# A recurrence on one Trainium2 core: y's matmuls in two groups, centring by a matmul, loads in other places, and output weights that are split once and read back split

## The chip, the core and the metric

The kernel runs on one core of one Trainium2 chip. The metric is device microseconds of one execution of the whole program. TensorE (PE) does matmuls into PSUM; VectorE (DVE) and ScalarE (ACT) work elementwise and are the ones that read PSUM here; GpSimd (POOL) works elementwise in SBUF and issues some DMAs; SyncE (SP) issues most DMAs, in the order of the program. All data are float32. A product of a weight and an activation is made of three matmuls, since both are split into a high and a low part (`h` and `l`): `wh*xh`, `wl*xh`, `wh*xl`.

## What is computed

One step of a two-layer decoder for a prompt of 1040 tokens and for 8 single tokens that share all weights. Layer 0 is retention and an RG-LRU, layer 1 is RWKV-7; each is followed by a gated ConvFFN. The change lies in layer 1, whose core is this recurrence over tokens, for 16 heads of 64:

```
def rwkv7_step(S, inp):
    r_t, w_t, k_t, v_t, a_t, b_t = inp
    sa = jnp.einsum('bhij,bhj->bhi', S, a_t)
    S = S * w_t[:, :, None, :] + sa[..., None] * b_t[:, :, None, :] + v_t[..., None] * k_t[:, :, None, :]
    y = jnp.einsum('bhij,bhj->bhi', S, r_t)
    return S, y
...
    mu = jnp.mean(ys, axis=-1, keepdims=True)
    var = jnp.mean(jnp.square(ys - mu), axis=-1, keepdims=True)
    o = ((ys - mu) * lax.rsqrt(var + GN_EPS_C)).reshape(B, T, D) * gn_g + gn_b
    bonus = jnp.sum(rh * kh * r_k, axis=-1, keepdims=True) * vh
    o = (o + bonus.reshape(B, T, D)) * g
    return o @ p['w_o'], ...
```

## The kernel before

Layer 1 has two parts. `Layer1A` makes r, k, v and the gates, writes what the recurrence needs to scratch in DRAM (`d_kq`, `d_vt`, `d_gg`, `d_ab`), and steps the 8 sample tokens' states (`samp_pair`, eight times for two heads each). `Layer1B` then runs the recurrence in 17 chunks of 64 tokens. A chunk is two units of work, f=0 and f=1, each for four pairs of heads, so there are 34 units; here they are counted 0 to 33. The order of steps in a unit is a string: `UNIT = "pa z pt g1 u r r o r p2 g2 o o s o r y p3"`. Each letter calls one function:

- `pa`, `pt`, `p2`, `p3` prepare the next unit (`prep1` and so on). The 16 matmuls of `pa` (tile `A`) open a unit in the trace.
- `z`, `u`, `s`, `y` are the steps of the recurrence. `y` (function `yy`) makes 16 matmuls into one PSUM tile `y`: for each of four pairs of heads two that contract over 64 rows (`s0v` by `kq`) and then two that contract over 128 rows (`uv` by `ly`).
- `g1`, `g2` normalise the y of the unit before (`gn_unit`, `gn_unit2`): mean by a matmul with ones (`bones`), subtraction on DVE (L1847), Square on ACT, mean of squares by a matmul (L1857), a reciprocal root on ACT and DVE, the product (L1357), gains, and the split into `yh`, `yl`.
- `r` is one step of the inversion of 32x32 triangular matrices (`inv_steps`), elementwise work on DVE (L1440, L1442). It goes through four batches of matrices (a fifth was done before), each loaded from `d_ab` on POOL's queue; the load of the next batch stands with the last step of the batch before.
- `o` is a quarter of one output tile: 6 matmuls of 256 to 272 columns with `w_o` (`out_steps`). Four blocks of tokens, eight tiles each. The first three blocks are woven in, one tile to a unit: block 0 in units 9 to 16, block 1 in 17 to 24, block 2 in 25 to 32. The fourth runs behind the recurrence in `finish`, back to back, with matmuls for the next norm behind each tile.

Weights go through a queue `wq`: `load_next` issues a DMA of 512 KB into one of two buffers `wst`, `split_next` splits it into one of two pairs `wh`, `wl` (ACT L323, DVE L324) and calls `load_next`. At the first `o` of a tile `next_w` splits the weights of the tile after it. `w_o` is read and split again in each of the four blocks.

SP's order in a chunk: at the end of unit f=1 the set of 13 loads of the chunk after the next (`kq` of 1 MB first; it waits until y is done with the same buffer), then in unit f=0 one `wst`, `gg` of the next chunk, then in f=1 another `wst`. `p.x` (the residual, 4.3 MB) is read back from `d_x` at the start of the recurrence, behind the sets of chunks 0 and 1 and `gg` of chunk 0. The buffers of `Layer1A` lie in the same memory.

Of the kernel before, what the change touches and what calls it, by code (L numbers as in the profile page):

```python
# [44 lines left out]
def constants():  # L45

    f = np.float32
    c = {}
# [128 lines left out]
def unlayout(o):  # L177
# [21 lines left out]
       0.69, "v.s2": 1.38, "v.sum": 4.97, "v7.pair": 2.3, "v7.post": 8.2, "v7.post_d": 0.01, "v.fold": 1.57, "v.tr0":  # L199
# [848 lines left out]
class Layer1A:  # L1048
# [464 lines left out]
    def samp_pair(self, m):  # L1513
        nc = self.nc
        tt = (nc.vector if m == 7 else nc.gpsimd).tensor_tensor
        S, (a, w, b, k, r) = self.samp_tiles(m)
# [46 lines left out]
    def run(self, pool, done, first):  # L1563
# [24 lines left out]
        for name, tile, nxt, temps in stages:  # L1588
            for m in range(8):
                f, new = tile(m)  # L1590
                if name == "v":
# [7 lines left out]
                    if m == 7:  # L1599
                        new.append((POS["v7.pair"] - 6, lambda: (self.samp_pair(7), self.samp_sum(7))))  # L1600
# [32 lines left out]
def w_order_l1(io):  # L1633
# [3 lines left out]
    return o + [io["w_o"][m] for _ in OBLK for m in range(8)]  # L1637
# [9 lines left out]
class Layer1B:  # L1647
# [189 lines left out]
    def gn_unit(self, u):  # L1837
# [8 lines left out]
        nc.tensor.matmul(py[:, 1], lhsT=p.bones, rhs=yf, start=True, stop=True)  # L1846
        nc.vector.scalar_tensor_tensor(out=yf, in0=py[:, 1], scalar=-1.0 / 64, in1=yf, op0=OP.mult, op1=OP.add)  # L1847
        sq, v, y = new("sq"), new("v"), new("yr")
        nc.scalar.activation(out=sq, in_=yf, func=AF.Square)
# [37 lines left out]
    def run(self, pool):  # L1887
# [75 lines left out]
def build(tc, io):  # L1963
    nc = tc.nc
    with ExitStack() as ctx:
# [93 lines left out]
def scratch(pool):  # L2059
# [33 lines left out]
```

## Time and profile before

| what | us |
|---|---|
| median of 3 runs (3443.21 to 3454.74) | 3443.9 |
| the profiled execution, its own time | 3447.01 |
| its span in the trace | 3445.2 |
| recurrence, units 0 to 33 (from 2221.82 in the trace) | about 380 |
| output tiles of the last block, behind it | about 31 |

The page's second part shows PE at 9 tenths or more of nearly every slice outside the stretch from 1900 to 2330. In that stretch DVE and the DMA engines are busiest, and the granted clock of PE falls now and then. Matmul ends are modelled, so a busy PE is not one at its peak: whether PE or another engine sets the pace of a unit is read from the idle times in brackets and from the distance between the same instruction of two units.

### The profile page before, as it was taken

The page shows a single profiled execution, that of the slowest core. Times are in us where ns is not written, and L with a number is a line of the kernel's source. Part 1 is how long each engine was busy: PE and PEld are TensorE (multiplying, and loading weights), DVE is VectorE, ACT ScalarE, POOL GpSimd, SP SyncE. Part 2 cuts the span into 40 slices and gives each one's busy share as a digit, 9 for nine tenths or more (in the row PEclk, how much of TensorE's full clock was granted, in tenths as well). Part 3 has the DMA queues.
Part 4 walks back from the last instruction along what each step waited for, and adds up shares of the span by engine and source line. Part 5 has one row for each costly group of instructions (what it writes and reads, how often), then busy time and mean ns, then how long its engine had stood idle before and what let it go on. Part 6 is the DMA issues. An engine that isn't in the chain of part 4 may idle for free.

```text
span 3445.2 us, 55808 instructions
## 1 busy us (share of the span) xinstructions
PE 3272.4 (95%) x23480; PEld 3098.2 (90%) x23480; DVE 1709.7 (50%) x2850; ACT 1242.1 (36%) x2214; POOL 336.9 (10%) x645
## 2 busy tenths in 40 slices
PE   8999999999999999999997988779998999999998
PEld 7999989998999999999796888758887999999997
DVE  5434444556533333333766655678875433333334
ACT  4322224555422122121576444345564312213122
POOL 0100110100000000000101124312220000000000
PEclk9999999999999999999998989789999999999999
DMA  4111211111111111111254768976662111111111
GB/s 138 59 60 63 70 40 43 50 41 36 43 49 44 44 49 44 50 43 46 83 166 144 188 151 221 234 198 175 179 160 67 50 44 50 43 50 44 49 50 59
DMA packets 303066, 294.33 MB, mean 85 GB/s; under 512 B 233056, under 2 KB 248704, under 8 KB 300640
## 3 DMA queue, kind: packets, MB, share of 16 engines
q1 hardware_dynamic: 294368, 262.95, 26.3%
q0 software_dynamic: 8448, 27.82, 2.5%
q8 instruction: 185, 3.03, 0.4%
q14 instruction: 65, 0.53, 0.1%
HBM read 218.95 MB, written 67.47 MB: 83 GB/s over the span
## 4 chain that ended last, share of the span: by engine, by line
PE 32%; DVE 8%; ACT 4%; DMA 3%; issue 2%; SPq 2%; POOL 0%; DVEq 0%; ACTq 0%; POOLq 0%
PE d L335 9%; PE d L337 9%; PE d L336 9%; PE hs L1325 1%; DMA kq<-d_kq 1%; DVE xsl L324 1%; ACT wh L323 1%; DMA x<-d_pp 1%; PE A L1710 1%; PE nrm L429 1%; DVE x L1213 1%; DVE lz L1719 1%; DMA d_vt<-x 0%; SPq L1510 0%; PE y L1827 0%
## 5 line engine op out<-in xcount | busy, mean ns | idle before, releaser
L335 PE MATMUL d<-xsh,wh 128*128 128x350 f32 (+1 forms) x3656 | 1207.0, 330 | 11.7 <-ACT xsh L323 7.7
L337 PE MATMUL d<-xsl,wh 128*128 128x350 f32 (+1 forms) x3656 | 1193.7, 327 | 5.3 <-DVE xsl L324 5.2
L336 PE MATMUL d<-xsh,wl 128*128 128x350 f32 (+1 forms) x3656 | 1188.1, 325 | 4.3 <-DVE wl L324 4.3
L335 PEld LDWEIGHTS d<-xsh,wh 128*128 128x128 f32 x3656 | 695.9, 190 | 23.5 <-ACT xsh L323 9.1
L337 PEld LDWEIGHTS d<-xsl,wh 128*128 128x128 f32 x3656 | 694.7, 190 | 16.6 <-DVE xsl L324 15.8
L336 PEld LDWEIGHTS d<-xsh,wl 128*128 128x128 f32 x3656 | 696.7, 191 | 7.1 <-DVE wl L324 5.1
L335 PE MATMUL d<-T,wh 128*128 128x350 f32 (+1 forms) x1380 | 464.4, 337 | 15.8 <-DVE x L405 8.9
L324 DVE TENSOR_TENSOR wl<-wst,wh 128x1024 fp32r<-128x1024 f32 x248 | 303.4, 1224 | 331.8 <-ACT wh L323 329.5
L336 PE MATMUL d<-T,wl 128*128 128x350 f32 (+1 forms) x1380 | 445.6, 323 | 2.5 <-DVE wl L324 2.5
L337 PE MATMUL d<-T,wh 128*128 128x350 f32 (+1 forms) x1380 | 445.8, 323 | 1.4 <-DVE T L324 1.4
L323 ACT ACTIVATE wh<-wst 128x1024 fp32r<-128x1024 f32 x248 | 260.7, 1051 | 509.4 <-PE d L337 383.9
L405 DVE TENSOR_TENSOR x<-d,x 128x350 f32<-128x350 f32 (+1 forms) x450 | 230.3, 520 | 323.8 <-PE d L337 323.7
L991 DVE SCALAR_TENSOR_TENSOR T<-T,vec 128x1064 f32<-128x1064 f32 x88 | 116.8, 1327 | 398.2 <-ACT T L989 396.7
L335 PEld LDWEIGHTS d<-T,wh 128*128 128x128 f32 x1380 | 260.4, 189 | 28.4 <-DVE x L405 10.2
L336 PEld LDWEIGHTS d<-T,wl 128*128 128x128 f32 x1380 | 260.5, 189 | 10.0 <-DVE wl L324 3.2
L337 PEld LDWEIGHTS d<-T,wh 128*128 128x128 f32 x1380 | 260.5, 189 | 2.1 <-DVE T L324 2.1
L323 ACT ACTIVATE T<-T 128x1048 fp32r<-128x1048 f32 (+2 forms) x77 | 69.2, 899 | 288.1 <-DVE T L1004 241.2
L985 POOL TENSOR_SCALAR fcout<-T 128x2 f32<-128x2 f32 x44 | 11.2, 254 | 1515.3 <-ACT T L983 1515.3
L983 ACT ACTIVATE T<-d 128x350 f32<-128x350 f32 (+1 forms) x88 | 40.5, 462 | 269.6 <-PE d L337 269.6
L324 DVE TENSOR_TENSOR T<-T 128x1048 fp32r<-128x1048 f32 (+2 forms) x77 | 78.9, 1024 | 76.8 <-ACT T L323 76.8
L1004 DVE TENSOR_TENSOR T<-T,d 128x350 f32<-128x350 f32 x88 | 45.3, 515 | 120.4 <-PE d L337 120.4
L429 PE MATMUL nrm<-tmp,ones 128*128 128x350 f32 (+1 forms) x208 | 77.8, 479 | 15.4 <-ACT tmp L419 14.9
(410 smaller groups left out, 4090.4 us busy)
## 6 DMA issues: line engine op xcount, KB each, us to landing
wst<-in_w_up SPq DMA_DIRECT2D x88, 512.0 KB, 3.3
wst<-in_w_down SPq DMA_DIRECT2D x44, 512.0 KB, 3.4
wst<-in_w_in SPq DMA_DIRECT2D x40, 512.0 KB, 3.2
kq<-d_kq SPq DMA_DIRECT2D x17, 1024.0 KB, 5.5
wst<-in_w_o SPq DMA_DIRECT2D x32, 512.0 KB, 4.2
T<-d_sv SPq DMA_DIRECT2D x80, 128.0 KB, 3.9
d_kq<-x SPq DMA_DIRECT2D x16, 544.0 KB, 4.2
d_kq<-x SPq DMA_DIRECT2D x32, 272.0 KB, 5.3
```

Source lines behind the costliest of these rows:

```text
L323: self.nc.scalar.activation(out=h, in_=src, func=AF.Copy)
L324: (eng or self.nc.vector).tensor_tensor(out=l, in0=src, in1=h.bitcast(F32), op=OP.subtract)
L335: mm(ps, lhsT=h, rhs=a, start=start and j == 0, stop=False)
L336: mm(ps, lhsT=l, rhs=a, start=False, stop=False)
L337: mm(ps, lhsT=h, rhs=b, start=False, stop=stop and j == n - 1)
L405: self.nc.vector.tensor_tensor(out=xv, in0=ps, in1=xv, op=OP.add)
L429: self.nc.tensor.matmul(self.nps[tb][:, :n], lhsT=self.ones, rhs=sq, start=m == 0, stop=m == 7)
L983: nc.scalar.activation(out=ub[:, 18 + c0:18 + c1], in_=ps, func=AF.Copy)
L991: nc.vector.scalar_tensor_tensor(out=c, in0=ub[:, j:1064 + j], scalar=w[j], in1=c, op0=OP.mult, op1=OP.add)
L1004: nc.vector.tensor_tensor(out=st["f"][:, c0:c1], in0=c[:, 16 + c0:16 + c1], in1=ps, op=OP.mult)
L1213: nc.vector.tensor_tensor_scan(L, self.rst, s, 0.0, OP.mult, OP.add)
L1325: self.nc.tensor.matmul(ps[:, 2 * i:2 * i + 2], lhsT=v[:, c0:c0 + 128], rhs=self.p.bones[:, 0:128:64], start=True, stop=True)
```

## The change

Six edits, all around the recurrence.

1. In `yy` the eight matmuls over 64 rows of a unit stand first, then the eight over 128 rows. Only the first pair of them starts the accumulation.
2. A constant `centre` (identity minus ones/64, by heads) joins `masks`. `gn_unit` multiplies y by it, so that PSUM holds y less its mean. The subtraction on DVE is gone; Square reads PSUM, and the last product of `gn_unit2` reads PSUM too.
3. `w_o` is split once. In block 0 the pair `wh`, `wl` is written to scratch (`d_wo`, 1 MB a tile) after the split; in blocks 1 to 3 `split_next` reads both halves back by two DMAs of 512 KB straight into `wh` and `wl`. No `wst` load, no split there.
4. The residual is read back in three parts, behind the sets of loads at the end of chunks 1, 4 and 7.
5. The load of the next batch of matrices to invert (on POOL's queue, with a small memset of POOL behind it) stands four steps earlier.
6. The last sample pair's first three products go from DVE to POOL; its value part is a function of its own, run later.

```
     def split_next(self):
         t, n, pre = self.loaded.pop(0)
+        again = pre is not None and pre[0] == "again"
...
-        if pre is not None:
-            self.scale_w(t, *pre)
-        self.split(t, h, l)
+        if again:
+            for i, v in enumerate((h, l)):
+                self.nc.sync.dma_start(out=v.bitcast(F32), in_=t[i])
+        else:
...
+            self.split(t, h, l)
+            if pre is not None and pre[0] == "keep":
+                for i, v in enumerate((h, l)):
+                    self.nc.sync.dma_start(out=pre[1][i], in_=v.bitcast(F32))
         self.load_next()
...
-    return o + [io["w_o"][m] for _ in OBLK for m in range(8)]
+    return o + [(io["w_o"][m], ("keep", d["wo"][m])) if b == 0 else (d["wo"][m], ("again",))
+                for b in range(len(OBLK)) for m in range(8)]
...
-                nc.tensor.matmul(py[r, m, :], lhsT=t["s0v"][r, g, h, :], rhs=t["kq"][r, g, 3, :], start=True, stop=False)
+                nc.tensor.matmul(py[r, m, :], lhsT=t["s0v"][r, g, h, :], rhs=t["kq"][r, g, 3, :], start=m == 0, stop=False)
+        for m in range(4):
+            g = 4 * f + m
             for h in range(2):
                 r = slice(h * 64, h * 64 + 64)
-                nc.tensor.matmul(py[r, m, :], lhsT=t["uv"][:, g, h, :], rhs=w["ly"][:, h, m, :], start=False, stop=True)
+                nc.tensor.matmul(py[r, m, :], lhsT=t["uv"][:, g, h, :], rhs=w["ly"][:, h, m, :], start=False, stop=m == 3)
...
-        nc.tensor.matmul(py[:, 1], lhsT=p.bones, rhs=yf, start=True, stop=True)
-        nc.vector.scalar_tensor_tensor(out=yf, in0=py[:, 1], scalar=-1.0 / 64, in1=yf, op0=OP.mult, op1=OP.add)
+        nc.tensor.matmul(py[:, 1], lhsT=p.centre, rhs=yf, start=True, stop=True)
...
-        nc.scalar.activation(out=sq, in_=yf, func=AF.Square)
+        nc.scalar.activation(out=sq, in_=py[:, 1], func=AF.Square)
...
-        self.a.rs_mul(yf, v, y, sq)
+        self.a.rsq(v, y, sq)
+        nc.vector.tensor_tensor(out=yf, in0=py[:, 1], in1=sq, op=OP.mult)
...
-        for c0, c1 in TBS:
-            nc.sync.dma_start(out=p.x[:, :, c0:c1], in_=self.d["x"][:, :, c0:c1])
...
-                last, ahead = inv.pop(), s[0]
-                inv.append(lambda last=last, ahead=ahead: (ahead(), last()))
+                step, ahead = inv[-5], s[0]
+                inv[-5] = lambda step=step, ahead=ahead: (ahead(), step())
...
+                if c in (1, 4, 7):
+                    c0, c1 = TBS[c // 3]
+                    nc.sync.dma_start(out=p.x[:, :, c0:c1], in_=self.d["x"][:, :, c0:c1])
```

On DVE, a unit of block 1 before, from the mask of tile A to the product that ends g2's root (`pr`, `mt` are steps of the inversion):

```order
L1719 TENSOR_TENSOR lz<-A,masks 64x4x64 x2
L1722 TENSOR_TENSOR ly<-A,masks 128x256 x2
L1847 SCALAR_TENSOR_TENSOR yf<-y,yf 128x256
L1440 TENSOR_TENSOR pr<-mt 128x234
L1442 TENSOR_TENSOR mt<-mt,pr 128x18x13
L1440 TENSOR_TENSOR pr<-mt 128x228
L1442 TENSOR_TENSOR mt<-mt,pr 128x19x12
L324 TENSOR_TENSOR wl<-wst,wh 128x1024
L1440 TENSOR_TENSOR pr<-mt 128x220
L1442 TENSOR_TENSOR mt<-mt,pr 128x20x11
L1351 SCALAR_TENSOR_TENSOR sq<-sq,v 128x256
L1352 SCALAR_TENSOR_TENSOR sq<-sq,yr 128x256
```

The same unit on DVE in the changed kernel:

```order
L1742 TENSOR_TENSOR lz<-A,masks 64x4x64 x2
L1745 TENSOR_TENSOR ly<-A,masks 128x256 x2
L1453 TENSOR_TENSOR pr<-mt 128x234
L1455 TENSOR_TENSOR mt<-mt,pr 128x18x13
L1453 TENSOR_TENSOR pr<-mt 128x228
L1455 TENSOR_TENSOR mt<-mt,pr 128x19x12
L1453 TENSOR_TENSOR pr<-mt 128x220
L1455 TENSOR_TENSOR mt<-mt,pr 128x20x11
L1364 SCALAR_TENSOR_TENSOR sq<-sq,v 128x256
L1365 SCALAR_TENSOR_TENSOR sq<-sq,yr 128x256
L1884 TENSOR_TENSOR yf<-y,sq 128x256
```

The subtraction and the weight split are gone, and the last product now reads `y`, so the next unit's y matmuls, which write that PSUM tile again, come behind it.

On SP, the end of a set of loads and what follows it up to the next set, in block 1 before:

```order
L1691 DMA uv<-d_vt 64x8x64
L276 DMA wst<-in_w_o 128x1024
L1696 DMA gg<-d_gg 128x1024
L276 DMA wst<-in_w_o 128x1024
L1671 DMA kq<-d_kq 128x2048
```

The same stretch of SP's queue in the changed kernel:

```order
L1714 DMA uv<-d_vt 64x8x64
L291 DMA wh<-d_wo 128x1024
L291 DMA wl<-d_wo 128x1024
L1719 DMA gg<-d_gg 128x1024
L291 DMA wh<-d_wo 128x1024
L291 DMA wl<-d_wo 128x1024
L1694 DMA kq<-d_kq 128x2048
```

Where the raw weights of a tile three further on were loaded, both halves of the next tile's weights are loaded now; the pair behind the set is issued in unit f=0 and first used at the first `o` of unit f=1.

## Rows read from the trace of the kernel before

**Rows 1.** The page's first part, PE: busy us, share, instructions.

```profile
PE 3272.4 (95%) x23480; PEld 3098.2 (90%) x23480; DVE 1709.7 (50%) x2850; ACT 1242.1 (36%) x2214; POOL 336.9 (10%) x645
```

**Rows 2.** Stretches: start, units 0-2, 3-8, 9-16, 17-32; last: clock, DMA, GB/s.

```profile
2196.00:2221.82 25.82, 11.64 (x94) 9.53 (x92) 15.27 (x39) 6.08 (x15) 5.20 (x13) 0.66 0.98 250
2221.82:2261.06 39.24, 28.85 (x421) 22.64 (x417) 23.18 (x64) 15.23 (x45) 5.81 (x8) 0.67 0.96 268
2261.06:2326.55 65.49, 55.08 (x841) 41.48 (x841) 49.22 (x134) 32.45 (x94) 12.85 (x20) 0.81 0.60 153
2326.55:2415.90 89.35, 88.10 (x1316) 72.89 (x1312) 73.23 (x181) 52.60 (x135) 17.74 (x28) 0.98 0.67 175
2415.90:2591.30 175.40, 171.27 (x2631) 141.66 (x2625) 135.83 (x331) 106.07 (x274) 35.69 (x52) 1.00 0.62 167
```

**Rows 3.** PE's timeline: starts of six units, idle before and releaser in brackets.

```profile
2261.06 1.22 PE L1710 MATMUL A<-kq 64*128 64x128 f32 x8 [6.31 <-DMA kq<-d_kq]
...
2326.55 2.08 PE L1710 MATMUL A<-kq 64*128 64x128 f32 x16
...
2339.00 1.16 PE L1710 MATMUL A<-kq 64*128 64x128 f32 x16
...
2427.24 1.16 PE L1710 MATMUL A<-kq 64*128 64x128 f32 x16
...
2570.00 1.16 PE L1710 MATMUL A<-kq 64*128 64x128 f32 x16
...
2580.65 1.16 PE L1710 MATMUL A<-kq 64*128 64x128 f32 x16
```

**Rows 4.** Timeline of unit 18, which starts at 2427.24, several engines.

```profile
2430.57 0.39 PE L335 MATMUL d<-yh,wh 128*128 128x256 f32 x1
...
2431.47 0.41 DVE L1847 SCALAR_TENSOR_TENSOR yf<-y,yf 128x256 f32<-128x256 f32 x1
...
2432.38 0.70 PE L1857 MATMUL y<-sq,masks 128*128 128x256 f32 x2 [0.46 <-ACT sq L1849]
...
2434.43 0.69 PE L1797 MATMUL s<-uv,bk 128*64 128x64 f32 x16
...
2434.69 0.47 ACT L1858 ACTIVATE v<-y,gneps 128x256 f32<-128x256 f32 x1
...
2435.94 0.33 PE L1824 MATMUL y<-kq,s0v 64*64 64x64 f32 x4
...
2436.20 0.34 PE L1827 MATMUL y<-ly,uv 128*64 128x64 f32 x4
...
2437.01 0.43 DVE L1357 TENSOR_TENSOR yf<-yf,sq 128x256 f32<-128x256 f32 x1
```

**Rows 5.** SP's timeline: first load of a set, and the weight load behind it.

```profile
2426.71 0.32 SPq L1671 DMA_DIRECT2D kq<-d_kq  x1
...
2436.61 0.56 SPq L276 DMA_DIRECT2D wst<-in_w_o  x1
...
2515.27 0.32 SPq L1671 DMA_DIRECT2D kq<-d_kq  x1
...
2527.62 0.56 SPq L276 DMA_DIRECT2D wst<-in_w_o  x1
```

**Rows 6.** Views of tile wst (512 KB), then kq (1 MB): their last lines.

```profile
DMA to landing us min/median/max: 3.3/3.8/4.4
...
DMA to landing us min/median/max: 5.2/5.5/11.3
```

**Rows 7.** DVE's timeline in unit 5: first inversion step of a batch.

```profile
2292.29 0.19 DVE L1440 TENSOR_TENSOR pr<-mt 128x30 f32<-128x30 f32 x1 [3.79 <-DMA mt<-d_ab]
```

**Rows 8.** SP's timeline near the start: the residual's three loads.

```profile
2239.84 4.02 SPq L1897 DMA_DIRECT2D x<-d_x  x3
```

**Rows 9.** The chain of waits in the last block: norm matmuls behind two tiles.

```profile
2617.79 0.59 PE nrm L429 x2
...
2621.39 0.59 PE nrm L429 x2
```

More of the change, by code (lines that the diff above doesn't have):

```diff
@@ L198 @@
        "k7.bonus": 4.69, "k7.amat": 4.82, "k7.store_ab": 5.7, "v.fill": -0.43, "v.gate": -2.73, "v.s0": -0.33, "v.s1":
-       0.69, "v.s2": 1.38, "v.sum": 4.97, "v7.pair": 2.3, "v7.post": 8.2, "v7.post_d": 0.01, "v.fold": 1.57, "v.tr0":
+       0.69, "v.s2": 1.38, "v.sum": 4.97, "v7.pair": 2.3, "v7.value": 8.15, "v7.post": 8.2, "v7.post_d": 0.01, "v.fold": 1.57, "v.tr0":
        0.82, "v.tr1": 1.27, "v.tr2": 1.5, "v.store_v": 2.12, "v.store": 5.18, "v.pair": 0.82, "v.load": 5.27, "v.inv":
@@ L273, in load_next @@
             src, pre = w if isinstance(w, tuple) else (w, None)
+            if pre is not None and pre[0] == "again":
+                self.loaded.append((src, None, pre))
+                return
             n = src.shape[-1]
@@ L280, in split_next @@
         t, n, pre = self.loaded.pop(0)
+        again = pre is not None and pre[0] == "again"
+        n = 1024 if again else n
         h = self.wsp.tile([128, 1024], F32R, tag="wh", name="wh")[:, :n]
         l = self.wsp.tile([128, 1024], F32R, tag="wl", name="wl")[:, :n]
[L283 to L285 removed]
+        if again:
+            for i, v in enumerate((h, l)):
+                self.nc.sync.dma_start(out=v.bitcast(F32), in_=t[i])
+        else:
+            if pre is not None and pre[0] != "keep":
+                self.scale_w(t, *pre)
+            self.split(t, h, l)
+            if pre is not None and pre[0] == "keep":
+                for i, v in enumerate((h, l)):
+                    self.nc.sync.dma_start(out=pre[1][i], in_=v.bitcast(F32))
         self.load_next()
@@ L1514, in samp_pair @@
         nc = self.nc
-        tt = (nc.vector if m == 7 else nc.gpsimd).tensor_tensor
         S, (a, w, b, k, r) = self.samp_tiles(m)
+        tt = nc.gpsimd.tensor_tensor
         bc = lambda v: v.unsqueeze(2).to_broadcast([128, NS, 64])
@@ L1523, in samp_pair, with samp_value @@
         tt(out=S, in0=S, in1=b, op=OP.add)
+        if m < 7:
+            self.samp_value(m)
+    def samp_value(self, m):
+        nc = self.nc
+        S, (a, w, b, k, r) = self.samp_tiles(m)
+        tt = (nc.vector if m == 7 else nc.gpsimd).tensor_tensor
+        bc = lambda v: v.unsqueeze(2).to_broadcast([128, NS, 64])
         tt(out=k, in0=k, in1=bc(self.smp["v"][:, m, :]), op=OP.mult)
@@ L1599, in run @@
                     if m == 7:
-                        new.append((POS["v7.pair"] - 6, lambda: (self.samp_pair(7), self.samp_sum(7))))
+                        new.append((POS["v7.pair"] - 6, lambda: self.samp_pair(7)))
+                        new.append((POS["v7.value"] - 6, lambda: (self.samp_value(7), self.samp_sum(7))))
                         new += [(POS["v7.post"] - 6 + POS["v7.post_d"] * i, g) for i, g in enumerate(self.samp_post())]
@@ L1975, in build @@
         xt = p.x = const.tile([128, 8, T], F32, name="x")
-        masks = const.tile([128, 536], F32, name="masks")
+        masks = const.tile([128, 664], F32, name="masks")
         p.ones = const.tile([128, 128], F32, name="ones")
@@ L1979, in build @@
         p.ident, p.causal, p.mask0 = masks[:, 0:128], masks[:, 128:256], masks[:24, 256:280]
-        p.rwmask, p.bones = masks[:, 280:408], masks[:, 408:536]
+        p.rwmask, p.bones, p.centre = masks[:, 280:408], masks[:, 408:536], masks[:, 536:664]
         with tc.manual_schedule():
-            p.wq += w_order_l0(io) + w_order_ffn(io, 0) + w_order_l1(io) + w_order_ffn(io, 1)
+            d = scratch(pool)
+            p.wq += w_order_l0(io) + w_order_ffn(io, 0) + w_order_l1(io, d) + w_order_ffn(io, 1)
             c0, c1 = TBS[0]
@@ L2063, in scratch @@
               "ab": [NCH, 16, 2, 32, 32], "mt": [NCH, 16, 2, 32, 32], "mm": [NCH, 16, 2, 32, 32], "sv": [5, 16, NS, 64]}
-    return {n: dr.tile(sh, F32, name="d_" + n) for n, sh in shapes.items()}
+    t = {n: dr.tile(sh, F32, name="d_" + n) for n, sh in shapes.items()}
+    t["wo"] = dr.tile([8, 2, 128, 1024], F32, name="d_wo")
+    return t
 def ffn_phase(p, H, l, wv, pool, cost, emit):
```

6 lines of the change are left out of this document (3 added, 3 removed).

## The prediction, made before the changed kernel had run

> **What bounds the kernel now.** I read the page's first part first: PE is busy for 95% of the span [rows 1]. That only says that the other engines are second over the whole; how far PE really sets the pace has to be read stage by stage. So I read the table of stretches next [rows 2]. It shows four regimes in the recurrence. In units 0 to 2 the DMA engines are at 0.96 and PE's granted clock is 0.67; the stretch ahead is the same (0.98, 0.66). In units 3 to 8 PE counts 55.08 of 65.49 us, DVE 49.22, clock 0.81: several engines wait for one another. In units 9 to 16 and 17 to 32 PE counts 98% of the time with the clock at 0.98 and 1.00, DVE 82% and 77%. There PE sets the pace, but DVE is close behind. Third, PE's timeline [rows 3]: unit 32 begins 10.65 us after unit 31 (2570.00 to 2580.65), by which time the inversion is done, and the mean of units 17 to 32 is 175.40/16 = 10.96, of units 9 to 16 89.35/8 = 11.17. I take 10.65 as PE's own time for a unit. Nothing outside the recurrence and the tiles behind it is touched except a little of `Layer1A`'s end.
>
> **y in two groups.** Where shapes alternate, four instructions start 0.26 us after the four before (2435.94, 2436.20), and their busy time is 0.33, so 0.07 is the tail [rows 4]. A unit's y has eight such groups, 8 x 0.26 = 2.08. Sixteen instructions of one shape take 0.69 (step `s`), less the tail 0.62; grouped, y should take 2 x 0.62 = 1.24. That is 0.84 less on PE in each unit: 10.65 becomes 9.8. It counts in full only where PE sets the pace.
>
> **Centring by a matmul.** DVE loses the 0.41 us subtraction; PE's wait for Square, 0.46 us in unit 18, shrinks, since Square can start right behind the matmul [rows 4]. In exchange the last product of g2 reads the PSUM tile that the same unit's y then writes. PE stands at y until DVE is done with that product; behind it on PE are p3 and the next unit's A, so every such wait is a whole delay. Bounds: ACT's `v` starts at 2434.69 and the product ends at 2437.01 + 0.43, so 2.75 us pass from `v` on [rows 4]. `v` starts 2.31 after the second bones matmul (2432.38), but in unit 18 ACT's weight split stood ahead of it; I estimate, from the 0.70 us of that matmul, that without a split it starts 0.75 after it. Then the product ends 3.5 us after that matmul starts, and PE reaches y 2435.94 - 2432.38 = 3.56 after it. It just fits. I allow 0.05 and take 9.85 a unit; if `v` comes as late as it does in unit 18 (2.31), y waits 1.5 us and the gain of the grouping is gone.
>
> **Start of the recurrence.** The residual (4.3 MB) stands in SP's queue ahead of what follows [rows 8], and at unit 2 PE sits 6.31 us until `kq` lands [rows 3]. With the residual gone that wait goes. Against this, the `keep` write of tile 0 puts 1 MB more into a stretch that moves 250 to 268 GB/s [rows 2], 4.2 us if all of it shows; I take 2.5. Sum **-4** (-7 to -2). The sample pair on POOL, 128 more columns of masks and the scratch declared earlier: nothing, since unit 0 is released by its `kq` and POOL is busy for 10% only [rows 1]. If that cover fails it costs a microsecond or two once.
>
> **Units 3 to 8.** The 3.79 us in which DVE waits for the next batch of matrices [rows 7] goes with the load four steps earlier, and in a stretch that DVE helps to set six subtractions of 0.41 [rows 4] go: 3.8 + 2.5 = **-6.3**. If the PE clock (0.81) stays low more often, as little as -1; with some of y's gain, -9.
>
> **Units 9 to 16.** Here tiles are still split, and now also written back. DVE without the subtraction would give 11.17 - 0.41 = 10.76; PE alone 9.8. DVE's other work, 73.23/8 - 0.41 = 8.7 a unit, fits in neither as idle-free time, so I stay near the DVE end, 10.6: 8 x 0.57 = **-4.5** (-3 to -10). The writes go through SP, which waits for the split; what is queued behind is the next raw weight load, which waited for that split before too. DMA share 0.67 [rows 2] leaves room for 1 MB a unit.
>
> **Units 17 to 32.** Without any stall 16 x (10.96 - 9.85) = -17.8. But the weights have a new path. In a chunk SP issues the set of 13 loads first, its `kq` when the first half of y has been through (0.62 after y begins, call that Y), and the thing behind the set follows 9.90 us later (2426.71 to 2436.61), once 12.35 [rows 5]. Before, that thing was a raw load for a tile three further on, so nobody waited. Now it is the pair for the first `o` of the coming f=1 unit. The trace has no load of a pair; the nearest row is `kq`, as large (1 MB), whose landing takes 5.2 at least and 5.5 in the median; a 512 KB load takes 3.8 [rows 6], which would be the other end if the halves ran side by side. I take 5.2: the pair is there at Y + 0.62 + 9.90 + 5.2 = Y + 15.7. PE needs it at Y, plus the rest of the unit (10.96 - (2435.94 - 2427.24) = 2.26, less y's 0.84: 1.4), plus the f=0 unit of 9.85, plus 3.33 to the first `o` (2427.24 to 2430.57) [rows 4]: Y + 14.6. So PE stalls about 1.1 us in each of eight chunks, 9 in all, and about 3 more once where a third of the residual (1.4 MB) stands ahead of the pair. Sum -17.8 + 9 + 3 = **-5.8** (-17.8 with no stall; +15 with 12.35 and 5.5, a stall of 3.9 in each chunk).
>
> The Trainium skill, page DMA: Bandwidth & Descriptors, section Anatomy of one DMA — SWDGE (gpsimd) path, gives a DMA about 2.0 us plus its bytes at 436 GB/s, that is an estimate of 4.4 us for 1 MB; `kq`'s 5.2 to 5.5 here lies above it. By that rule the chunk's stall would be 0.3 and the whole about 3418; I go by the row.
>
> **Tiles behind the recurrence.** A tile takes 3.60 us there [rows 9]. With two pairs of buffers the pair of tile m+2 can be asked for only when tile m is through, and it lands 5.2 later, 1.6 after tile m+1 is through. Before, raw weights were two tiles ahead. Three such waits in eight tiles, since two tiles are then ready within one landing: **+4.8** (with 3.8, +0.6; with 5.5, +5.7).
>
> **The sum.** -4 - 6.3 - 4.5 - 5.8 + 4.8 = -16. The profiled execution took 3447.0, so 3431; the median of the runs shown is 3.1 lower, 3443.9, so I forecast **3428**.
>
> **Rivals.** (a) The loads hide. If SP comes to the pair earlier (the set's loads are quicker to issue with less traffic around) and a landing is nearer 3.8, the stalls (12) and the waits at the end (4.8) go: 3428 - 17 = **3411**. For it: the DMA share of units 17 to 32 is 0.62 [rows 2] and no raw weights are loaded there any more. Against it: 9.90 is SP's own row. (b) The change doesn't bring what it says: y's wait for DVE's product eats the grouping's 0.84, or the pair comes as late as 12.35 + 5.5. Then the units 17 to 32 stay at about 10.9, the term is 0 instead of -5.8, and units 9 to 16 give nothing: 3428 + 5.8 + 4.5 = **3438**, and up to 3450 with the +15. For it: DVE is within 23% of PE's time, and the product stands at the end of a chain over PE, ACT and DVE. (c) Slower: the stalls in the chunks drop PE's clock. After the 6.31 us wait the clock was low, and unit 9, which opens in the low state (its A takes 2.08 against 1.16), takes 12.45 us (2326.55 to 2339.00) [rows 3], about 1.65 over the 10.8 of a fast one by my estimate. If each chunk stalls by 3.9 and its next unit is as slow, the eight cost 8 x 1.65 = 13 on top of 3450: **3463**. It decides from the point where a chunk's stall nears 3.9; against it stands that a stall of 1.1 would follow from the median row, and that waits below 0.5 leave the clock at 1.00 in units 17 to 32 [rows 2].
>
> The Trainium skill, page TensorE: Matmul & The Clock Gate, section HAM oscillation — how this bites in real kernels, describes just that: a wait for a DMA in each step of a loop that brings the lower clock back at each step. In this trace only the start, with its waits of several microseconds, shows it.
>
> **How the numbers follow.** A measurement of this kernel can tell about 0.5%, 17 us, from no change; faster means below 3426.7. The forecast gets 0.40 and lies on that line, so half of it counts as faster. Rival (a) 0.30, faster. Rival (b) 0.21, no change. Rival (c) 0.09, slower. Faster 0.20 + 0.30 = 0.50, no change 0.20 + 0.21 = 0.41, slower 0.09. The range leaves out the slower rival and the far ends: low is (a) with 6 us more from units 9 to 16, 3405; high is (b) with part of the late pair, 3446.
>
> **What would show it.** y as two rows a unit of sixteen instructions, about 0.62 apart, in place of eight; no DVE subtraction; PE's A every 9.8 to 9.9 us in units 17 to 32, and the first `o` of the f=1 units idle for about 1 us behind a DMA of `wh` or `wl`; at y, PE's idle before it put down to DVE at most a few tenths. Behind the recurrence the norm matmuls 3.6 and 5.2 apart by turns. The 6.31 and the 3.79 us gone. What would make the number wrong: a longer or shorter way from the set's first load to the pair, y grouped that takes more than 1.3, a `v` that still comes late on ACT, and units 9 to 16 that still go by DVE.

## The result, and the profile after

The changed kernel takes 3467.4 us (median of 6 runs, 3458.0 to 3472.7) against 3447.1 for the kernel before (6 runs, 3442.2 to 3454.7). The ratio is 1.006, 95% interval 1.0045 to 1.0076: slower by 0.6%. The forecast was 3428, the range 3405 to 3446, so the time lies outside it and on the other side of no change. The profiled execution took 3472.7 against 3447.0, 25.7 us more.

The page's first part for the kernel after (busy us, share, instructions), beside [rows 1]:

```profile
PE 3263.3 (94%) x23480; PEld 3101.4 (89%) x23480; DVE 1670.1 (48%) x2789; ACT 1227.5 (35%) x2190; POOL 341.3 (10%) x648
```

PE, DVE and ACT have less to do than before (POOL 4.4 us more), and the kernel is slower. So the time has gone into waits. The table of stretches shows in which units; of after, these are units 0 to 2, 3 to 8, 9 to 16 and 17 to 32, the columns as in [rows 2]:

```profile
2230.36:2267.61 37.25, 27.40 (x421) 22.57 (x417) 21.20 (x60) 15.42 (x43) 4.29 (x7) 0.68 0.83 198
2267.61:2337.27 69.66, 50.33 (x844) 41.44 (x841) 48.96 (x133) 35.04 (x96) 14.61 (x22) 0.79 0.62 156
2337.27:2425.30 88.03, 82.85 (x1316) 70.76 (x1312) 69.16 (x171) 54.00 (x135) 17.89 (x28) 0.96 0.85 260
2425.30:2610.89 185.59, 167.62 (x2630) 141.91 (x2625) 111.88 (x299) 93.36 (x257) 36.01 (x52) 0.94 0.73 215
```

| stretch (profiled executions) | before | after | difference | forecast |
|---|---|---|---|---|
| up to unit 0 | 2221.82 | 2230.36 | +8.5 | with the next row -4 |
| units 0 to 2 | 39.24 | 37.25 | -2.0 | |
| units 3 to 8 | 65.49 | 69.66 | +4.2 | -6.3 |
| units 9 to 16 | 89.35 | 88.03 | -1.3 | -4.5 |
| units 17 to 32 | 175.40 | 185.59 | +10.2 | -5.8 |
| unit 33 and all behind it | 853.9 | 860.0 | +6.1 | +4.8 |

The 8.5 us ahead of unit 0 can't be put down to the change. Unit 0 begins anywhere from 2210.5 to 2230.4 in the fourteen profiles of this study, and one kernel whose program up to unit 15 is that of the changed kernel (`e3_early`) has it at 2213.7. What edit 6 moves lies ahead of unit 0 as well; no run has it alone. The other five rows add up to 17.2, near the 20.4 by which the medians differ. Below, stages are therefore compared from unit 0 on.

**Units 3 to 8.** PE's timeline in unit 3 after (start, us, engine, line, operation, idle before and its releaser): the matmul of g2, `s`, the two halves of y, and the next unit's A.

```profile
2272.26 0.70 PE L1881 MATMUL y<-sq,masks 128*128 128x256 f32 x2
2272.89 0.69 PE L1820 MATMUL s<-uv,bk 128*64 128x64 f32 x16
2276.35 0.99 PE L1847 MATMUL y<-kq,s0v 64*64 64x64 f32 x16 [2.78 <-DVE yf L1884]
2277.27 1.12 PE L1852 MATMUL y<-ly,uv 128*64 128x64 f32 x16
...
2278.89 1.65 PE L1733 MATMUL A<-kq 64*128 64x128 f32 x16
```

PE reaches y 1.3 us after g2's matmul starts and waits 2.78 for L1884, the product that now reads the PSUM tile. In the units that carry no `o`, nothing stands between g2 and y except `s`. Seven of the units 1 to 8 have this wait of 2.8, unit 4 one of 5.4. After the wait the clock is low: the halves of y take 0.99 and 1.12, where they take 0.68 and 0.69 below, and the A behind them 1.65 (up to 2.08 in the neighbours) against 1.16.

**Units 17 to 32.** The end of unit 20 and unit 21:

```profile
2473.28 0.68 PE L1847 MATMUL y<-kq,s0v 64*64 64x64 f32 x16
2473.89 0.69 PE L1852 MATMUL y<-ly,uv 128*64 128x64 f32 x16
...
2474.88 1.16 PE L1733 MATMUL A<-kq 64*128 64x128 f32 x16
...
2479.90 0.36 PE L348 MATMUL d<-yh,wh 128*128 128x256 f32 x1 [1.62 <-DVE mt L1455]
2481.09 0.40 PE L349 MATMUL d<-yh,wl 128*128 128x256 f32 x1 [0.83 <-DMA wl<-d_wo]
...
2481.50 0.41 PE L348 MATMUL d<-yh,wh 128*128 128x256 f32 x1
...
2485.34 0.28 PE L348 MATMUL d<-yh,wh 128*128 128x256 f32 x1
...
2488.89 1.16 PE L1733 MATMUL A<-kq 64*128 64x128 f32 x16
```

Grouped y is as forecast: two rows, 0.61 apart. The eight f=0 units take 9.91 or 9.92, against a forecast of 9.85. But the first `o` of unit 21 waits for `wh` and then for `wl`. (The first wait is put down to a step of DVE that ended just then; with the pairs issued earlier no wait stands there, though DVE's steps are the same, and in `e2_reload` the same wait is put down to `wh<-d_wo`.) Behind it the `o` matmuls take 0.41 in place of 0.28 for some 3 us. The unit takes 14.01, 4.1 over 9.92: 2.45 of idle time, and about 1.6 of the slower matmuls. The row of that unit beside the one of unit 19, where the wait is 0.81 (us, PE, PEld, DVE, ACT, POOL, clock, DMA share, GB/s):

```profile
2453.97:2464.96 10.99, 10.11 (x170) 8.47 (x164) 7.29 (x22) 5.83 (x17) 2.58 (x4) 1.00 0.77 264
2474.88:2488.89 14.01, 11.56 (x169) 9.69 (x165) 7.24 (x23) 5.82 (x17) 1.78 (x2) 0.88 0.64 212
```

The granted clock stays at 1.00 through the short wait and is 0.88 in the unit with the long one. The Trainium skill, page TensorE: Matmul & The Clock Gate, section HAM oscillation — how this bites in real kernels, describes a lower clock after each DMA wait of a loop; the trace agrees for unit 21 and shows none in unit 19.

Of the f=1 units, 17 takes 18.8, 21 14.0, 23 15.7, 29 13.7, the other four 10.8 to 11.3. Over 9.92 that is 27 us; without it the 16 units would have gained 16 x (10.96 - 9.92) = 16.6. The difference is about the +10.2 of the table. Of the 27, 17.1 are PE's waits at the first `o`: 6.4 in unit 17, 2.1 to 2.8 in units 21, 23 and 29, 0.6 to 1.1 in the other four. Another 8.7 are the rest of units 17, 21, 23 and 29, whose clock is 0.78 to 0.88; the other four units have it at 1.00.

SP's timeline (issue and its us) behind the residual's third part, and in the next two chunks; between them the matmul in unit 19 that waits for the pair:

```profile
2425.66 1.15 SPq L1958 DMA_DIRECT2D x<-d_x  x1
2426.85 0.95 SPq L291 DMA_DIRECT2D wh<-d_wo  x1
...
2443.18 0.32 SPq L1694 DMA_DIRECT2D kq<-d_kq  x1
...
2452.96 0.62 SPq L291 DMA_DIRECT2D wh<-d_wo  x1
2453.62 0.44 SPq L291 DMA_DIRECT2D wl<-d_wo  x1
2454.16 0.38 SPq L1719 DMA_DIRECT2D gg<-d_gg  x1
2454.64 0.38 SPq L291 DMA_DIRECT2D wh<-d_wo  x1
2455.06 0.49 SPq L291 DMA_DIRECT2D wl<-d_wo  x1
...
2458.50 0.38 PE L349 MATMUL d<-yh,wl 128*128 128x256 f32 x1 [0.81 <-DMA wl<-d_wo]
...
2464.08 0.32 SPq L1694 DMA_DIRECT2D kq<-d_kq  x1
...
2474.93 0.79 SPq L291 DMA_DIRECT2D wh<-d_wo  x1
```

The pair of unit 19 is issued 9.8 us behind the set's `kq`, as in [rows 5]; in six of the eight chunks it is 9.6 to 9.9, ahead of unit 21 10.9, and ahead of unit 17, behind the residual, 12.4. The next pair follows 1.7 us later, with `gg` between: five loads of 512 KB, 2.5 MB, within 2.6 us. PE's first matmul with `wl` starts when that half has landed, so the time from the issue of `wh` to it is what the pair takes: 5.5 us in unit 19 (2452.96 to 2458.50) and 6.2 in unit 21 (2474.93 to 2481.09). In units 17 to 31 it is 8.9, 5.5, 6.2, 7.4, 5.7, 5.4, 7.1 and 5.5. The landing itself is in the trace for two of these `wl`, those of units 21 and 29, in us from their own issue:

```profile
DMA to landing us min/median/max: 5.3/5.3/5.3
...
DMA to landing us min/median/max: 6.4/6.4/6.4
```

I had taken 5.2 for the whole pair. The Trainium skill, page DMA: Bandwidth & Descriptors, section Anatomy of one DMA — SWDGE (gpsimd) path, would give 512 KB an estimate of 3.2; the two landings here are 5.3 and 6.4, with other loads beside them, and the measurement decides.

**Behind the recurrence.** The chain of waits after (start, us, what), three of its rows:

```profile
2627.63 4.63 DMA wl<-d_wo
...
2635.90 4.51 DMA wl<-d_wo
...
2647.62 6.40 DMA wl<-d_wo
```

Where [rows 9] had only norm matmuls 3.60 apart, the chain now runs through the pairs' loads, as forecast: in PE's timeline the norm matmuls of five tiles stand 3.60, 4.57, 3.60 and 5.30 apart.

### The profile page after: what moved, and what is told of

Read it like the earlier page. It is cut to its first block, busy times and chain, and to the rows that moved or that the text cites. A ratio compares the mean times of both kernels' runs of the same rounds, so it can differ in the third digit from the quotient of the medians.

```text
span 3470.9 us, 55875 instructions
## 1 busy us (share of the span) xinstructions
PE 3263.3 (94%) x23480; PEld 3101.4 (89%) x23480; DVE 1670.1 (48%) x2789; ACT 1227.5 (35%) x2190; POOL 341.3 (10%) x648
## 4 chain that ended last, share of the span: by engine, by line
PE 34%; DVE 5%; DMA 5%; ACT 3%; SPq 2%; issue 2%; POOL 1%; DVEq 0%; ACTq 0%; POOLq 0%
PE d L348 9%; PE d L349 9%; PE d L350 9%; DMA wl<-d_wo 2%; PE hs L1338 1%; PE A L1733 1%; DMA kq<-d_kq 1%; DMA d_vt<-x 1%; DVE xsl L337 1%; DVE x L1226 1%; PE y L1847 1%; PE nrm L442 1%; SPq L1714 0%; PE y L1881 0%; DMA x<-d_pp 0%
## 5 line engine op out<-in xcount | busy, mean ns | idle before, releaser
L348 PE MATMUL d<-T,wh 128*128 128x350 f32 (+1 forms) x1380 | 464.2, 336 | 15.7 <-DVE x L418 8.7
L337 DVE TENSOR_TENSOR wl<-wst,wh 128x1024 fp32r<-128x1024 f32 x224 | 274.0, 1223 | 308.0 <-ACT wh L336 307.4
L336 ACT ACTIVATE wh<-wst 128x1024 fp32r<-128x1024 f32 x224 | 235.3, 1050 | 508.3 <-PE d L350 377.2
L348 PEld LDWEIGHTS d<-T,wh 128*128 128x128 f32 x1380 | 260.5, 189 | 28.1 <-DVE x L418 10.1
L348 PE MATMUL d<-yh,wh 128*128 128x256 f32 (+2 forms) x256 | 87.2, 341 | 10.7 <-DMA wh<-d_wo 6.6
```

Of the source, the lines that this page charges most:

```text
L336: self.nc.scalar.activation(out=h, in_=src, func=AF.Copy)
L337: (eng or self.nc.vector).tensor_tensor(out=l, in0=src, in1=h.bitcast(F32), op=OP.subtract)
L348: mm(ps, lhsT=h, rhs=a, start=start and j == 0, stop=False)
```

## The experiments

The stages of all kernels from their profiles (us; units 17 to 31 are 15 units; the last stage is unit 32 and all behind it), and the timed comparison with the kernel before. Each ratio is to executions of the kernel before taken beside that run, whose medians lie between 3442.0 and 3447.1; medians of different rows of the table can differ by as much without a cause in the kernel.

| kernel | units 0-2 | 3-8 | 9-16 | 17-31 | 32 to end | median | ratio, 95% interval |
|---|---|---|---|---|---|---|---|
| before | 39.2 | 65.5 | 89.4 | 164.8 | 864.6 | | |
| after | 37.3 | 69.7 | 88.0 | 175.7 | 869.9 | 3467.4 | 1.006 (1.0045 to 1.0076) |
| e1_raw | 38.7 | 70.4 | 85.4 | 157.2 | 865.1 | 3432.0 | 0.997 (0.995 to 0.9985) |
| e2_reload | 39.6 | 65.9 | 89.4 | 172.9 | 871.4 | 3460.2 | 1.005 (1.0031 to 1.0069) |
| e3_early | 38.5 | 70.6 | 85.2 | 152.3 | 866.7 | 3438.6 | 0.998 (0.9964 to 1.0001) |
| e4_early_raw3 | 37.5 | 70.6 | 89.9 | 151.0 | 864.1 | 3435.7 | 0.998 (0.9964 to 0.9993) |
| e10_x5 | 37.2 | 69.7 | 87.7 | 169.7 | 872.1 | 3456.6 | 1.004 (1.0022 to 1.0053) |
| e5_y | 39.1 | 63.5 | 88.6 | 163.9 | 865.1 | 3441.7 | 1.000 (0.9985 to 1.0009) |
| e6_centre | 38.3 | 83.0 | 96.0 | 170.8 | 866.5 | 3481.3 | 1.010 (1.0074 to 1.0123) |
| e8_hybrid | 34.2 | 62.2 | 86.6 | 152.5 | 869.5 | 3427.7 | 0.994 (0.9923 to 0.996) |
| e7_loads | 34.0 | 66.0 | 89.8 | 164.7 | 864.3 | 3442.3 | 0.999 (0.9979 to 1.0006) |
| e9_gap | 35.6 | 69.9 | 80.8 | 149.1 | 864.1 | 3424.6 | 0.994 (0.9923 to 0.9966) |
| e11_gap_hybrid | 34.5 | 62.2 | 79.7 | 149.2 | 862.3 | 3407.7 | 0.990 (0.9887 to 0.992) |
| e12_reload_best | 35.3 | 60.9 | 87.2 | 149.0 | 864.0 | 3423.1 | 0.994 (0.9917 to 0.9954) |

### The reload: undone, alone, issued earlier

`e1_raw`, the changed kernel without edit 3:

```
-    return o + [(io["w_o"][m], ("keep", d["wo"][m])) if b == 0 else (d["wo"][m], ("again",))
-                for b in range(len(OBLK)) for m in range(8)]
+    return o + [io["w_o"][m] for _ in OBLK for m in range(8)]
```

> The changed kernel with edit 3 undone: the raw output weights are loaded and split in each block, as before. Theory A (the reloaded pairs, issued behind the set of loads on SP, cost the 27 us of stalls that the changed kernel shows in units 17 to 32 at the first o of the f=1 units, and about 5 behind the recurrence): both go, the unit is a little over 9.92 since DVE and ACT split again, say 10.3, so units 17 to 32 take 165 against 185.6 and the tiles at the end about 31 again: about 3443. Rival B (the loss is the granted clock and the traffic around, not the place of the pairs): units 3 to 8 stay at about 69.7 and units 17 to 32 above 175; 3455 or more.

Measured: 3432.0. Units 17 to 31 take 157.2 against 175.7, each of them 10.48 or 10.49; behind them it is 865.1 against 869.9. Units 3 to 8 stay at 70.4. So without the reload the other five edits make the kernel faster, by 0.3% (0.15 to 0.5); the reload turned that into a loss.

`e2_reload`, the kernel before with edit 3 alone (its diff is that part of the diff above):

> The kernel before with edit 3 alone (write the split weights in block 0, read them back in blocks 1 to 3). Theory A: stalls at the first o of each f=1 unit from 17 on, about 20 us in all (the residual's third part does not stand ahead of the first pair here), plus 5 at the end, less 5 for the splits that are gone: about 3463 to 3467. Rival B: the reload by itself costs less than 5, 3443 to 3449, and the first o of the f=1 units does not wait for d_wo.

Measured: 3460.2, ratio 1.005, theory A by sign and nearly by size. Units 17 to 31 take 172.9, 8 more than before, with PE waiting for the pairs. In its unit 21, which takes 15.2:

```profile
2467.09 0.36 PE L347 MATMUL d<-yh,wh 128*128 128x256 f32 x1 [1.86 <-DMA wh<-d_wo]
2468.28 0.38 PE L348 MATMUL d<-yh,wl 128*128 128x256 f32 x1 [0.83 <-DMA wl<-d_wo]
```

The end is 6.8 longer. Units 3 to 8 are as before.

`e3_early`, the changed kernel with a pair issued as soon as its buffers are free:

```
             if i == OPART - 1:
...
                 nc.vector.tensor_tensor(out=xv, in0=st["ps"], in1=xv, op=OP.add)
+                if p.loaded and p.loaded[0][2] == ("again",):
+                    p.prefetch(2)
```

> The changed kernel with each reloaded pair issued right behind the last o of the tile that frees its buffers, so ahead of the set of loads and a unit earlier than before. Theory A: the waits for wh and wl at the first o go, the 16 units 17 to 32 take 9.9 each, 159 to 162 in all, the end stays as in the changed kernel: about 3440. Rival C (the pairs are late because the DMA queues move too much at once, wherever they are issued): the waits move to kq or stay, units 17 to 32 keep more than 175, 3455 or more.

Measured: 3438.6. Units 17 to 31 take 152.3, all of them 9.91 or 9.92 but unit 18 with 13.49, whose pair stands behind the residual's third part. The first `o` of unit 21, now without a wait:

```profile
2454.56 0.39 PE L348 MATMUL d<-yh,wh 128*128 128x256 f32 x1
```

The bytes are the same, and the same queue moves them. So the place in SP's order was the cost, 23 us, and not the traffic (rival C).

`e4_early_raw3` adds `... if b < 3 else io["w_o"][m]` to the list of weights, so that the last block has raw weights:

> As the kernel with early pairs, and the last block (the tiles behind the recurrence) takes the raw weights and splits them, as before. Theory A: the end goes back to about 31 us, 5 less than with early pairs: about 3435. If the end does not wait for the pairs (rival): the same time as with early pairs.

Measured: 3435.7, 2.9 less, and 2.6 less behind unit 32 in the profiles. The end did wait for the pairs, for less than the 5 expected, since with early pairs it is 866.7 already. As a difference of two medians this is within the spread of either, so it rests on the two profiles.

`e10_x5`, the changed kernel with the residual's parts in other chunks:

```
-                if c in (1, 4, 7):
-                    c0, c1 = TBS[c // 3]
+                if c in (1, 3, 5):
+                    c0, c1 = TBS[c // 2]
```

> The changed kernel with the residual's second and third part read behind the sets of chunks 3 and 5 in place of 4 and 7, so that none stands ahead of a reloaded pair. Theory A: unit 17, which took 18.8, takes 11 to 14 as the other f=1 units, the rest is as in the changed kernel: 5 to 8 less, about 3460. Rival: the first pair is late for another reason and unit 17 keeps 18 or more.

Measured: unit 17 takes 15.64 in place of 18.76, so the residual is 3.1 of it, the 3 of the forecast. It is not down to 11 to 14 as expected: without the residual too PE waits 3.3 there for the pair, and the unit's clock is 0.78. The median is 3456.6, 10 over the kernel before where after is 20 over it, which is more than these 3.1 explain; units 17 to 31 are 5.9 shorter in the profiles, where unit 23 gave another 2.4. Units 21, 23 and 29 are the long ones here as well (14.1, 13.4 and 13.1).

### y and the centring, each alone

`e5_y`, the kernel before with edit 1 alone:

> The kernel before with edit 1 alone (y's matmuls in two groups). By the changed kernel's own rows a grouped y takes 1.23 in place of 2.1. Theory D (PE sets the pace of units 17 to 32): the late units without inversion go from 10.65 to 9.8, units 17 to 32 from 175.4 to about 163, units 3 to 8 stay near 65: about 3428 if the rest is as before. Rival E (the gain of the grouping needs the centring by a matmul too): units 17 to 32 stay above 172, 3440 or more.

Measured: 3441.7, no difference. Units 17 to 31 take 163.9 against 164.8, where 15 x 0.84 = 12.6 was expected. This is rival E. PE's timeline in a late unit shows where the 0.84 went, to g2's matmul, which waits for Square behind DVE's subtraction:

```profile
2475.05 0.70 PE L1859 MATMUL y<-sq,masks 128*128 128x256 f32 x2 [0.99 <-ACT sq L1851]
```

That wait was 0.46 in [rows 4]. DVE comes to the subtraction only behind its inversion steps and the masks of A, and PE, done earlier, waited longer. In units 29 to 31, where the inversion is done, a unit takes 10.4 against 10.65, so there too the grouping alone brings 0.26 of its 0.84.

`e6_centre`, the kernel before with edit 2 alone:

> The kernel before with edit 2 alone (centring by a matmul). Theory D (y has to wait for DVE's last product, which reads the PSUM tile; where no o stands between g2 and y that wait is 2.8 to 5.4 us a unit and the granted clock falls): units 3 to 8 go from 65.5 to about 70, with A at 2.08 in most of them and PE's wait at y put down to DVE; units 17 to 32 are paced by that chain, about 11.3 a unit against 10.96: about 3455. Rival F (centring by a matmul costs nothing, and the low clock of units 3 to 8 comes from y's grouping or from the loads): units 3 to 8 at 63 to 66, 3444 or less.

Measured: 3481.3, the slowest of all. The row of its units 3 to 8, and PE's wait at y in one of them (unit 6) and in a late unit:

```profile
2265.61:2348.65 83.04, 67.32 (x841) 51.45 (x841) 48.77 (x132) 34.87 (x96) 15.21 (x24) 0.64 0.50 126
```

```profile
2317.12 0.33 PE L1825 MATMUL y<-kq,s0v 64*64 64x64 f32 x4 [2.78 <-DVE yf L1860]
...
2476.22 0.33 PE L1825 MATMUL y<-kq,s0v 64*64 64x64 f32 x4 [0.65 <-DVE yf L1860]
```

Theory D, and stronger than I had it: 17.5 us more in units 3 to 8 where 5 were expected, with the clock at 0.64 against 0.81. PE's waits there add up to 15.7 us against 10.1 in the kernel before, so the longer part of the 17.5 goes with the lower clock. The late units come to 11.37, as expected (11.3).

`e8_hybrid`, the kernel with early pairs, and the old centring where no `o` is woven in:

```
+        early = 2 * c + f < 8
-        nc.tensor.matmul(py[:, 1], lhsT=p.centre, rhs=yf, start=True, stop=True)
+        nc.tensor.matmul(py[:, 1], lhsT=p.bones if early else p.centre, rhs=yf, start=True, stop=True)
...
+        if early:
+            nc.vector.scalar_tensor_tensor(out=yf, in0=py[:, 1], scalar=-1.0 / 64, in1=yf, op0=OP.mult, op1=OP.add)
-        nc.scalar.activation(out=sq, in_=py[:, 1], func=AF.Square)
+        nc.scalar.activation(out=sq, in_=yf if early else py[:, 1], func=AF.Square)
```

> The kernel with early pairs, with the old centring (subtraction on DVE, product from SBUF) for the y of units 0 to 7, where no o is woven in. Theory D: y no longer waits for DVE in units 1 to 8, the clock of units 3 to 8 rises, 63 to 66 in place of 70.6, all else the same: 5 us less than with early pairs alone, about 3434. Rival F: units 3 to 8 stay near 70, same time as with early pairs alone.

Measured: 3427.7, ratio 0.994. Its units 3 to 8:

```profile
2244.69:2306.86 62.17, 50.97 (x845) 40.49 (x840) 51.29 (x140) 32.64 (x96) 14.59 (x22) 0.78 0.71 178
```

They take 62.2 against 70.6, and units 0 to 2 go from 38.5 to 34.2 as well, which I had not counted. In units 1 to 8 y no longer waits for DVE; its longest wait is 0.4, for ACT's `v`. That settles the early units: the wait of y for DVE's product is their loss. The clock over the stretch is not higher, as I had expected it to be (0.78 against 0.79 with early pairs), so it was the wait more than the clock.

### The loads alone

`e7_loads`, the kernel before with edits 4 and 5 alone:

> The kernel before with edits 4 and 5 alone (the residual's loads moved, the load of the next matrices four steps earlier). What was predicted: the 6.31 us wait of PE for kq in unit 2 and the 3.79 us wait of DVE for d_ab in unit 5 go, units 0 to 2 take about 34 in place of 39.2, units 3 to 8 about 61 in place of 65.5: about 3436. Rival: the waits go and others take their place (DVE's inversion steps stand in a row, kq still lands late); units 0 to 8 keep more than 102 of their 104.7, 3441 or more.

Measured: 3442.3, no difference that the runs can tell. Units 0 to 2 take 34.0 against 39.2, the forecast's 34. Units 3 to 8 are 66.0, as before, where 61 was expected, and unit 5 takes 14.25 with the earlier load as without. DVE's wait of 3.79 is gone from its timeline. PE's timeline in that unit, first one row of the kernel before and then three of this run:

```profile
2285.16 0.46 PE L1734 MATMUL Tp<-masks,kq 64*128 64x64 f32 x8 [2.57 <-ACT mt L1761]
...
2281.85 0.46 PE L1734 MATMUL Tp<-masks,kq 64*128 64x64 f32 x8 [2.56 <-ACT mt L1761]
...
2285.71 1.22 PE L1857 MATMUL y<-sq,masks 128*128 128x256 f32 x2 [0.63 <-ACT sq L1849]
...
2291.76 2.08 PE L1710 MATMUL A<-kq 64*128 64x128 f32 x16
```

In both kernels PE first waits 2.6 for ACT, ahead of the place of DVE's wait, and then goes on at the low clock (1.22 and 2.08 for 0.70 and 1.16), so it is as late without DVE's wait as with it. The wait was not on the path.

### The split behind g2

In `e1_raw` a unit takes 10.48 and not 9.92. PE's wait there, and ACT's order ahead of it:

```profile
2480.26 0.68 PE L1846 MATMUL y<-kq,s0v 64*64 64x64 f32 x16 [0.64 <-DVE yf L1883]
```

```profile
2475.64 1.06 ACT L336 ACTIVATE wh<-wst 128x1024 fp32r<-128x1024 f32 x1
...
2477.30 0.48 ACT L1881 ACTIVATE v<-y,gneps 128x256 f32<-128x256 f32 x1
```

This is the "`v` that still comes late" of the prediction: ACT's split stands ahead of `v`. `e9_gap` is `e1_raw` with the split of the next tile put behind the products of g2:

```
+    def gn_unit2(self, u, split=False):
...
+        if split:
+            p.prefetch(1)
         p.split(y3[:, :, 0:n], yh[:, 4 * f:4 * f + 4, o:o + n], yl[:, 4 * f:4 * f + 4, o:o + n])
...
-                st["w"], st["ps"] = p.next_w(), p.bank()[:, :c1 - c0]
+                st["w"], st["ps"] = p.next_w(1 if b == 3 else 0), p.bank()[:, :c1 - c0]
```

> The changed kernel with raw weights in each block (edit 3 undone), and the split of the next tile's weights moved from the first o to the place behind the last products of g2, where ACT waits 2.4 us for DVE. Theory G (with raw weights the unit takes 10.48 because ACT's split stands ahead of v, so that DVE's product comes late for y): the unit goes to 9.92, units 9 to 32 take 24 x 0.56 = 13 less, about 3418. Rival H (the split costs the same anywhere, since DVE or ACT is full): 10.4 or more a unit, 3430 or more.

Measured: 3424.6, and 9.91 to 9.95 for nearly all units from 10 on. In the profiles units 9 to 31 take 12.7 less than in `e1_raw`, as expected; the ratios, 0.997 and 0.994, are less far apart. ACT's timeline, and PE's y in the same unit, now without a wait:

```profile
2475.24 0.47 ACT L1881 ACTIVATE v<-y,gneps 128x256 f32<-128x256 f32 x1
...
2476.19 0.42 ACT L1363 ACTIVATE sq<-yr 128x256 f32<-128x256 f32 x1
2476.52 1.04 ACT L336 ACTIVATE wh<-wst 128x1024 fp32r<-128x1024 f32 x1
```

```profile
2478.20 0.68 PE L1846 MATMUL y<-kq,s0v 64*64 64x64 f32 x16
```

Theory G. DVE and ACT have room for the split; only its place was wrong.

`e11_gap_hybrid` joins this with the old centring of units 0 to 7:

> As the kernel with the split behind g2, with the old centring for the y of units 0 to 7. Theory D and G together: units 3 to 8 at 62 in place of 70, units 17 to 32 at 9.92: about 3410. If G is wrong, about 3423; if D does not add, as the kernel with the split behind g2 alone.

Measured: 3407.7, ratio 0.990 (0.9887 to 0.992), the fastest of all. Its units 3 to 8, 9 to 16, 17 to 32:

```profile
2251.91:2314.11 62.20, 49.97 (x845) 39.65 (x841) 51.34 (x140) 32.70 (x96) 14.59 (x22) 0.81 0.70 177
2314.11:2393.83 79.72, 79.38 (x1318) 67.71 (x1313) 70.90 (x176) 54.46 (x138) 18.30 (x28) 1.00 0.76 208
2393.83:2552.97 159.14, 157.49 (x2631) 134.46 (x2626) 128.53 (x315) 108.43 (x273) 35.87 (x52) 1.00 0.69 193
```

PE counts 99% of units 9 to 32 at the full clock.

`e12_reload_best` keeps the reload, with early pairs, raw weights in the last block, the residual behind chunks 1, 3 and 5, and the old centring of units 0 to 7:

> The reload kept at its best: early pairs in blocks 1 and 2, raw weights in the last block, the residual's parts behind chunks 1, 3 and 5, old centring for units 0 to 7. Theory A and D: units 17 to 32 at 159 without a stall, the end at 31, units 3 to 8 at 62: about 3423, some 4 less than early pairs with old centring alone. Beside the kernel with the split behind g2: if that reaches 9.92 too, the reload gains nothing over it.

Measured: 3423.1. Units 17 to 31 take 149.0, the same as 149.2 with raw weights. Units 9 to 16, where the pairs are split ahead of `v` and written, take 87.2 against 79.7. So even at its best the reload gains nothing in the units it serves. (The reload with block 0's split behind g2 was not run.)

## Why the prediction was wrong, point by point

- **y in two groups.** Right in size: 1.23 a unit against the 1.24 forecast, and 9.92 a unit against 9.85 where nothing else waits. Wrong in what it needs: I held the 0.84 to count wherever PE sets the pace, and took [rows 3] for PE's own pace. Alone it brought nothing (`e5_y`), since DVE and ACT were as close; it pays only with DVE's subtraction gone.
- **Centring by a matmul.** This step failed. I priced the new wait (the product ends 3.5 us after g2's matmul starts, PE comes to y 3.56 after it) in unit 18, which has three `o` between g2 and y, and used the result for all units. Units 0 to 8 have none; by [rows 4] PE comes to y some 1.3 after g2 there, which makes a wait of about 2.2 in each. The trace has 2.78, and 5.4 in unit 4, where the inversion's steps stand ahead of the product on DVE. PE's waits in units 3 to 8 add up to 19.3 us, all of them at y, where the kernel before has 10.1. So these units went +4.2 instead of -6.3. `e6_centre` and `e8_hybrid` show the mechanism from both sides. The other end that I named, the late `v`, was right: 0.64 of wait, 10.48 a unit, in `e1_raw`.
- **Start.** The 6.31 us wait went, as forecast. Units 0 to 2 gave 2.0 and not more, as the same wait of y stands in them: with the old centring they are 4 us shorter (`e8_hybrid`), with the loads alone 5 (`e7_loads`).
- **The d_ab wait.** The wait went, its 3.79 did not count: PE was late for other reasons in that unit (`e7_loads`).
- **Units 9 to 16.** -1.3 against -4.5, in the profile of after, where unit 13 opens with a wait of 1.1 for `kq` and at the low clock. Two more profiles have the same program up to unit 15: -4.2 (`e3_early`) and +0.5 (`e4_early_raw3`). So one profile can't tell the forecast from nothing here, and why single units of 11 to 12 us stand among the others stays open. Those others take 10.48, near my 10.6, but by luck: I put 10.6 down to DVE's load, and it is y's wait of 0.5 to 0.6 behind ACT's split, as `e9_gap` shows with 9.92.
- **Units 17 to 32.** This is the larger part of the miss, +10.2 against -5.8, and the step that failed is the sum of the stalls. The path was right: SP came to the pair 9.6 to 9.9 behind `kq` in six chunks, and PE waited at the first `o` of every f=1 unit; in units 19, 25, 27 and 31 by 0.6 to 1.1, where 1.1 was forecast. Two of its terms were wrong. I took one landing of 5.2 for all eight pairs: they took 5.4 to 5.7 in those four units, 6.2 to 7.4 in units 21, 23 and 29 and 8.9 in unit 17, behind the residual, and SP came later to two of them. That makes 17.1 us of waits where I had 12. And I put the lower clock behind a stall at nothing: it cost another 8.7 in units 17, 21, 23 and 29. Over 9.92 a unit the sum is 27. Rival (c) had that fall of the clock, but only from a stall of 3.9 on; in unit 29 it came with 2.1. The kernel before has it already behind the wait of 2.57 in its unit 5.
- **Behind the recurrence.** +4.8 forecast, +5.4 from unit 32 on, and 4.8 more than in `e1_raw`, which lacks only the reload. The other kernels with the reload in the last block have +2 to +8 there.

Why some pairs take 5.5 us and others 7, in units that are alike in the program, stays open. Ahead of units 21 and 29 POOL issues writes of inverted matrices (1 MB from 2468.93, 0.25 MB from 2560.08), and in unit 23 the issue of `wl` takes 1.85 us, but no run here took one of these away.

## What to carry to other kernels

When an operation that used to read SBUF is made to read PSUM, the next writer of that tile waits for it: price that wait in every kind of unit, the emptiest first, not in the one that is easiest to read. An edit that relieves one of two engines that run neck and neck can show nothing alone, as `e5_y` did, so price it together with the one that relieves the other, and expect to lose if one of them also adds a wait. Before replacing work by a transfer, look whether the work only stands in the wrong place of its queue: here the split, moved by a few instructions, cost nothing, and a load that was moved ahead of a set of others cost 23 us less.

## What the runs showed of the hardware

In the kernel after, waits of 2.1 us and more at the first `o` were followed by matmuls at the lower of the two clock levels (1.2 GHz: in unit 21 a 256-column matmul every 0.21 us for some 3 us, in place of 0.12; granted clock of these units 0.78 to 0.88), and waits of 1.1 and less were not (1.00). The border is not sharp between runs: a wait of 1.24 was followed by it in unit 17 of `e2_reload` (0.88), one of 1.38 in unit 25 of `e10_x5` was not (1.00). Two loads of 512 KB that had others of that size issued beside them took 5.3 and 6.4 us, where the 3.3 to 4.4 of [rows 6] come from two loads, one at the end of the recurrence and one behind it. And the start of unit 0 moves by up to 20 us from profile to profile, without a change in the program that explains it, so that stages had to be compared one by one.
